# A two-layer hybrid decoder on one core: the low parts of the mixing's weights kept in device memory for the second half of the sequence

## The chip, the core and the metric

The kernel runs on one core of a Trainium2 chip. The metric is device time in microseconds of one execution (lower is better). TensorE is called PE here (PEld is its loading of weights), VectorE is DVE, ScalarE is ACT, GpSimd is POOL and SyncE is SP. SP computes nothing: it issues nearly all DMAs of this kernel, in one queue, in order.

## The reference: what is computed

Two layers over 1024 positions of width 1024, in float32. Cut to what matters:

```python
for l in range(DEPTH):                                   # DEPTH = 2
    shift_m, scale_m, gate_m, shift_f, scale_f, gate_f = split(silu(c) @ ada_w[l] + ada_b[l], 6)
    h = rms_norm(x, g_pre_mix[l]) * (1.0 + scale_m) + shift_m
    q, k, v, u = split(h @ w_in[l] + b_in[l], ...)       # 512, 128, 128 and 512 columns
    attn_out = sliding_window_attention_with_sinks(rotary(q), rotary(k), v, sinks[l])
    pool_out = causal_pool_mixer(u, pool_w[l], pool_scale[l])
    mix = concatenate([attn_out, pool_out], axis=-1) @ w_out[l]
    x = x + gate_m * rms_norm(mix, g_post_mix[l])
    h = rms_norm(x, g_pre_ffn[l]) * (1.0 + scale_f) + shift_f
    f = (silu(h @ w_gate[l]) * (h @ w_up[l])) @ w_down[l]      # inner width 2816
    x = x + gate_f * rms_norm(f, g_post_ffn[l])
```

## The kernel before

**Three products for one.** To keep float32's accuracy with fast matmuls, each operand is split into a high part (ACT rounds it, L220) and a low part (DVE subtracts the high part from the original, L221), and `mm3` (L263, L266, L267) sums high by high, high by low and low by high into one PSUM bank.

**Two halves.** The sequence is worked on in two halves of 512 positions, h = 0 and 1. Each weight tile of the mixing, 128 x 512 floats (256 KB), is therefore used twice in a layer: 8 tiles for the queries (`q_rows`), 4 for keys and values (`kv_rows`), 8 for the pooling's input (`u_rows`) and 16 for the output projection (`wsrc` in `mix_out`), 36 in all. `weight` fetches such a tile: SP loads it into a `raw` tile (L233), and `split` makes `hi` and `lo` of it. It is called anew for each half, so that loading, rounding and subtraction are done 72 times in a layer. `one_ahead` asks for the tile of the next step before the matmuls of this one are written.

**Buffers.** `part` hands out pieces of 512 columns: two `raw` tiles of 2048, three `hi` tiles and three `lo` tiles of 1024 columns. A piece can be written again when all that use its whole tile are done. The pooling mixer's operands and some left operands of the output projection take `lo` pieces too.

**Stages of a layer's mixing**, with the times of layer 0 in the profile:
- first queries, keys and values (q0, kv0; to about 57 us);
- the "dense" stage (to about 158 us): pooling input of half 0 (u0), then queries, keys and values of half 1 (q1, kv1), with the attention of half 0 and its pooling written between them;
- out0 (to about 215 us): output projection of half 0 in two rounds of 8 tiles, beside the first attention blocks of half 1;
- u1 (to about 250 us): pooling input of half 1; the feed-forward's first products follow it, among them out1 (about 305 to 350 us), the output projection of half 1.

**The modulation beside it.** The columns of `ada_w` that this layer still needs are summed on DVE in the dense stage and in out0: `ada_sum` loads tiles `ar` of 256 KB through SP (L306) into two buffers and adds them up (`ada`, L296 and L298). When 8 tiles are summed, the sum is split (`ph<-ada`), and `close` has PE reduce it over the partitions (L412 and L413, or L469 and L470). `after(ins, recent["split"])` keeps each such sum behind the low part that was written last before it.

A scheduler puts the instructions of each engine in order at build time. Each engine then runs its own list strictly in order and waits at semaphores. In the second half, the instruction that needs a free `lo` piece is DVE's subtraction; the SP queue holds loads of `raw`, `ar` and the residual, and stores.

Of the kernel before, what the change touches and what calls it, by code (L numbers as in the profile page):

```python
# [11 lines left out]
F32 = mybir.dt.float32  # L12
# [3 lines left out]
AF = mybir.ActivationFunctionType  # L16
# [4 lines left out]
P = 128  # L21
# [7 lines left out]
ATT = NH * HD  # L29
KVW = NKV * HD  # L30
QK = ATT + KVW
QKV = ATT + 2 * KVW
POOLW = D - ATT
INW = QKV + POOLW
# [32 lines left out]
def hybrid_decoder_kernel(  # L67
# [22 lines left out]
    nc = tc.nc  # L90
# [5 lines left out]
    dr = ctx.enter_context(tc.tile_pool(name="dr", bufs=1, space=DRAM))  # L96
# [19 lines left out]
    def t_(tag, shape, dt=F32):  # L116
        if tag in SMALL:
            return small.tile(shape, dt, tag=tag, name=tag, bufs=SMALL[tag])
        if tag in SHARED:
            return sb.tile(shape, dt, tag=tag, name=tag, bufs=SHARED[tag])  # L120
        return now["pool"].tile(shape, dt, tag=tag, name=tag, bufs=REGIONS[now["name"]][tag])
# [3 lines left out]
    def part(tag, n=512):  # L125

        tile_, used = now.get(tag, (None, WIDE[tag]))
        if used + n > WIDE[tag]:
            tile_, used = t_(tag, [P, WIDE[tag]], F32 if tag == "raw" else F32R), 0
        now[tag] = (tile_, used + n)  # L130
        return tile_[:, used : used + n]
# [84 lines left out]
    recent = {}  # L216

    def split(hi, lo, src):

        a = nc.scalar.activation(hi, src, AF.Copy)  # L220
        v = nc.vector.tensor_sub(lo, src, hi.bitcast(F32))  # L221
        for ins, prev in zip((a, v), recent.get("hold", ())):
            after(ins, prev)
        recent["cast"], recent["split"] = a, v

    def weight(*srcs):

        raw = part("raw")
        for psl, view, src in srcs:
            dst = raw[psl]  # L230
            if view:
                dst = dst.rearrange("p (a b) -> p a b", a=view)
            nc.sync.dma_start(dst, src)  # L233
        hi, lo = part("hi"), part("lo")
        split(hi, lo, raw)
        return hi, lo

    def after(ins, prev):
        tc.add_manual_dep(
            ins.ins, prev.ins.name,  # L240
            mybir.DependencyInfo(mybir.DependencyClass.NoSync, mybir.DependencyReason.DATA),
            reason="order on the same engine",
        )
# [15 lines left out]
    ALLP = slice(0, P)  # L259
# [404 lines left out]
    def natural_proj(fn, left, wsrc, ss, G):  # L664

        K = len(left)  # L670
        lows = {}
        for nh in range(2):
            cs = slice(nh * 512, (nh + 1) * 512)
            banks = [acc_bank() for _ in range(NT)]
            for k in range(K):
                wh, wl = weight(*wsrc(k, nh))
                lh = part("hi")
                if k in lows:
                    ll = lows[k]
                    nc.scalar.activation(lh, left[k], AF.Copy)  # L680
                else:
                    if nh == 0 and k < 6:
                        lows[k] = t_("uT" if k < 4 else "pt", [P, UW], F32R)[:, :T]
                    ll = lows[k] if k in lows else part("lo")
                    split(lh, ll, left[k])
                for t in range(NT):
                    mm3(banks[t], lh[:, tiles[t]], ll[:, tiles[t]], wh, wl, k == 0, k == K - 1)
                yield
            for t in range(NT):
                square_sum(ss, t, nh, banks[t])  # L690
                nc.vector.tensor_mul(fn[t][:, cs], banks[t], G[:, cs])  # L691
# [21 lines left out]

    def kv_rows(l, k):
        return weight(
            (ALLP, 2, w_in[l, k * P : (k + 2) * P, ATT:QKV].rearrange("(a p) n -> p a n", p=P))
        )

    def q_rows(l, k):
        return weight((ALLP, None, w_in[l, k * P : (k + 1) * P, 0:ATT]))  # L720

    def u_rows(l, k):
        return weight((ALLP, None, w_in[l, k * P : (k + 1) * P, QKV:INW]))

    def all_rows(rows, l, step=1):
        return [lambda k=k: rows(l, k) for k in range(0, KD, step)]
# [295 lines left out]
    def mix_out(l, cats, G):  # L1022
        order = [*range(GRP, KD), *range(GRP)]
        left = [cats[k // 4][:, k % 4, :] for k in order]

        def wsrc(i, nh):
            k = order[i]
            cs = slice(nh * 512, (nh + 1) * 512)
            if k < GRP:
                return (  # L1030
                    (slice(0, HD), None, w_out[l, k * HD : (k + 1) * HD, cs]),
                    (slice(HD, P), None, w_out[l, (GRP + k) * HD : (GRP + k + 1) * HD, cs]),
                )
            return ((ALLP, None, w_out[l, k * P : (k + 1) * P, cs]),)

        fn = [t_("fn", [P, D]) for _ in range(NT)]
        ss = t_("ss", [P, 8])
        return fn, ss, natural_proj(fn, left, wsrc, ss, G)
# [346 lines left out]
    scaled = normalise(xs, rstd, cs=FIRST_COLS[0], hold=(recent["row"], recent["hot"]))  # L1385
    recent["hold"] = recent["square"], scaled
    ask_q = one_ahead(all_rows(q_rows, 0))
    recent.pop("hold")

# [20 lines left out]
    queries0 = q_pass(0, hts[0], par, qkvs0, ask_q, second_piece)  # L1410
    normalise(xs, rstd, cs=FIRST_COLS[1], hold=recent["hold"])
    keys0 = kv_pass(0, hts[0], par, qkvs0, one_ahead(all_rows(kv_rows, 0, 2)), (pv, msc_bank()))
    NB0 = len(FIRST_BLOCKS)
    sums = None
# [36 lines left out]
    for l in range(DEPTH):  # L1451
# [14 lines left out]
        def dense0():  # L1466
            yield from q_pass(l, hts[0], par, qkvs[0], ask) if l else queries0
            yield from kv_pass(l, hts[0], par, qkvs[0], ask) if l else keys0

        ask = one_ahead(  # L1470
            (all_rows(q_rows, l) + all_rows(kv_rows, l, 2) if l else [])
            + all_rows(u_rows, l) + all_rows(q_rows, l) + all_rows(kv_rows, l, 2)
        )
        side = ada_jobs(l)
# [43 lines left out]
        ]  # L1518
        pre = first_half()
        ask1 = one_ahead(all_rows(u_rows, l))  # L1520
        run(u_pass(l, 1, pieces, cols, uts[1], lambda k, ins: None, ask1), KD, (att, 10), (pre, NT + 2 + KD))
        pool = pool_mix(l, 1, uts[1], cols, cats[1][1])
# [138 lines left out]
```

## Time and profile before

| | us |
|---|---|
| median of 3 runs | 1906.01 (1905.44 to 1906.4) |
| span of the profiled execution, first to last instruction | 1904.4 |
| PE busy in it | 1864.7 (98%) |
| DVE busy | 1540.4 (81%) |
| ACT busy | 948.4 (50%) |
| POOL busy | 20.0 (1%) |
| moved by DMA | 341.86 MB, 180 GB/s in the mean |

For the profiled execution the page gives the span alone; the median of the timed runs lies 1.6 us above it. PE's matmuls overlap and their ends are modelled, so that 98% is not PE at its best pace: the pace has to be taken from the distance between two matmuls' starts. The shares are means over stages that differ; the mixing's stages are read one by one.

### The profile page before, as it was taken

The page shows a single profiled execution, that of the slowest core. Times are in us where ns is not written, and L with a number is a line of the kernel's source. Part 1 is how long each engine was busy: PE and PEld are TensorE (multiplying, and loading weights), DVE is VectorE, ACT ScalarE, POOL GpSimd, SP SyncE. Part 2 cuts the span into 40 slices and gives each one's busy share as a digit, 9 for nine tenths or more (in the row PEclk, how much of TensorE's full clock was granted, in tenths as well). Part 3 has the DMA queues.
Part 4 walks back from the last instruction along what each step waited for, and adds up shares of the span by engine and source line. Part 5 has one row for each costly group of instructions (what it writes and reads, how often), then busy time and mean ns, then how long its engine had stood idle before and what let it go on. Part 6 is the DMA issues. An engine that isn't in the chain of part 4 may idle for free.

```text
span 1904.4 us, 26019 instructions
## 1 busy us (share of the span) xinstructions
PE 1864.7 (98%) x8954; PEld 1540.3 (81%) x8954; DVE 1540.4 (81%) x2889; ACT 948.4 (50%) x1791; POOL 20.0 (1%) x67
## 2 busy tenths in 40 slices
PE   7999999999999999999999999999999999999998
PEld 5887788888888788888888868888887888888886
DVE  7899886668898888788879988846888888867687
ACT  4875795654222223445558667845622222234452
POOL 0000000000000000000000000000000000000000
PEclk9999999999999999999999989999999999999999
DMA  9345563655555665944554464536654565574343
GB/s 341 112 144 161 161 221 125 191 172 193 194 183 188 205 210 172 320 143 150 172 179 139 126 181 164 178 111 209 214 189 146 198 216 197 199 249 157 117 141 114
DMA packets 229540, 341.86 MB, mean 180 GB/s; under 512 B 17016, under 2 KB 126472, under 8 KB 229408
## 3 DMA queue, kind: packets, MB, share of 16 engines
q1 hardware_dynamic: 228800, 338.10, 53.8%
q10 hardware_dynamic: 576, 2.10, 0.3%
q8 instruction: 70, 1.15, 0.3%
q14 instruction: 62, 0.51, 0.1%
q0 software_dynamic: 32, 0.00, 0.0%
HBM read 267.25 MB, written 72.89 MB: 179 GB/s over the span
## 4 chain that ended last, share of the span: by engine, by line
PE 80%; DVE 10%; DMA 5%; ACT 3%; issue 2%; SPq 0%; DVEq 0%; ACTq 0%; POOL 0%; POOLq 0%
PE acc L263 25%; PE acc L266 24%; PE acc L267 24%; DMA ar<-in_ada_w_dram 2%; DVE lo L221 1%; DVE ada L298 1%; DMA raw<-in_w_up_dram 1%; PE msc L904 1%; PE msc L561 1%; ACT hi L220 1%; PE pv L263 1%; PE pv L266 1%; PE pv L267 1%; ACT raw L554 1%; DVE fn L1162 1%
## 5 line engine op out<-in xcount | busy, mean ns | idle before, releaser
L220 ACT ACTIVATE hi<-raw 128x1024 fp32r<-128x1024 f32 (+1 forms) x388 | 331.8, 868 | 360.1 <-PE acc L266 197.1
L221 DVE TENSOR_TENSOR lo<-raw,hi 128x1024 fp32r<-128x1024 f32 (+1 forms) x388 | 380.2, 987 | 121.3 <-ACT hi L220 116.4
L263 PE MATMUL acc<-t,hi 128*128 128x512 f32 x704 | 274.6, 390 | 2.7 <-ACT hi L220 2.6
L266 PE MATMUL acc<-t,hi 128*128 128x512 f32 x704 | 274.0, 389 | 0.0
L267 PE MATMUL acc<-t,lo 128*128 128x512 f32 x704 | 271.8, 389 | 0.0
L263 PE MATMUL acc<-bh,hi 128*128 128x512 f32 x520 | 202.8, 390 | 0.0
L267 PE MATMUL acc<-bh,lo 128*128 128x512 f32 x520 | 202.4, 389 | 0.0
L263 PE MATMUL acc<-hT,hi 128*128 128x512 f32 x480 | 190.2, 396 | 0.6 <-DVE fn L691 0.6
L266 PE MATMUL acc<-hT,hi 128*128 128x512 f32 x480 | 188.4, 392 | 0.0
L267 PE MATMUL acc<-hT,lo 128*128 128x512 f32 x480 | 187.6, 392 | 0.0
L1162 DVE TENSOR_TENSOR fn<-acc,fn 128x512 f32<-128x512 f32 x220 | 150.3, 685 | 38.2 <-PE acc L267 37.6
L263 PEld LDWEIGHTS acc<-t,hi 128*128 128x128 f32 x704 | 132.2, 188 | 32.1 <-ACT hi L220 5.1
L267 PEld LDWEIGHTS acc<-t,lo 128*128 128x128 f32 x704 | 132.2, 188 | 28.7 <-DVE lo L221 1.2
L266 PEld LDWEIGHTS acc<-t,hi 128*128 128x128 f32 x704 | 132.2, 188 | 27.1
L266 PE MATMUL acc<-ph,hi 128*128 128x512 f32 x320 | 124.7, 390 | 0.0
L1098 ACT ACTIVATE fn<-fn 128x512 f32<-128x512 f32 x44 | 27.9, 633 | 181.7 <-DVE fn L1162 181.7
L263 PEld LDWEIGHTS acc<-bh,hi 128*128 128x128 f32 x520 | 97.6, 188 | 20.2
L267 PEld LDWEIGHTS acc<-bh,lo 128*128 128x128 f32 x520 | 97.6, 188 | 20.2
L298 DVE SCALAR_TENSOR_TENSOR ada<-ar,c_act,ada 128x512 f32<-128x512 f32 x140 | 104.6, 747 | 10.1 <-DMA ar<-in_ada_w_dram 9.7
L263 PE MATMUL acc<-hi 128*128 128x512 f32 x256 | 103.5, 410 | 2.4 <-DVE fn L691 2.0
L263 PEld LDWEIGHTS acc<-hT,hi 128*128 128x128 f32 x480 | 90.2, 188 | 19.2 <-DVE fn L691 1.4
L267 PEld LDWEIGHTS acc<-hT,lo 128*128 128x128 f32 x480 | 90.1, 188 | 18.6 <-issue 0.2
(323 smaller groups left out, 3814.5 us busy)
## 6 DMA issues: line engine op xcount, KB each, us to landing
ar<-in_ada_w_dram SPq DMA_DIRECT2D x160, 256.0 KB
raw<-in_w_gate_dram SPq DMA_DIRECT2D x44, 512.0 KB
raw<-in_w_up_dram SPq DMA_DIRECT2D x44, 512.0 KB
raw<-in_w_in_dram SPq DMA_DIRECT2D x80, 256.0 KB
raw<-keeps SPq DMA_DIRECT2D x40, 512.0 KB
keeps<-fn SPq DMA_DIRECT2D x66, 256.0 KB
two_b<-in_w_down_dram SPq DMA_DIRECT2D x30, 512.0 KB
raw<-keepa SPq DMA_DIRECT2D x25, 512.0 KB
```

Source lines behind the costliest of these rows:

```text
L220: a = nc.scalar.activation(hi, src, AF.Copy)
L221: v = nc.vector.tensor_sub(lo, src, hi.bitcast(F32))
L263: ins = nc.tensor.matmul(dst, lh, rh, start=first, stop=False)
L266: nc.tensor.matmul(dst, lh, rl, start=False, stop=False)
L267: return nc.tensor.matmul(dst, ll, rh, start=False, stop=last)
L298: ins = nc.vector.scalar_tensor_tensor(acc, w, c_act[:, i : i + 1], acc, op0=ALU.mult, op1=ALU.add)
L554: nc.scalar.activation(hf, bank, AF.Identity, bias=shift, scale=scale)
L561: ins = nc.tensor.transpose(bank[:, t * P : (t + 1) * P], src[t], ident)
L904: nc.tensor.transpose(bank[:, i * P : (i + 1) * P], s[:, ii, ck * P : (ck + 1) * P], ident)
L1098: nc.scalar.activation(g, g, AF.Silu)
L1162: nc.vector.tensor_add(halves_of(dst)[m], bank, halves_of(src)[m])
```

## The change

The first call of `weight` for a tile now also stores the low part to a buffer in device memory, by a DMA in POOL's queue. The second call, for half 1, loads the low part from there by SP, into its `lo` piece, and only ACT's rounding is left to compute. Tiles are told apart by a key; both layers use the same 36 buffers. The tile of the weight itself is loaded in both halves, as before. In all 72 stores and 72 loads of 256 KB come in, and 72 subtractions of 128 x 512 on DVE go (20 of them lie in q1, kv1 and u1 of each layer, 16 in out1).

```diff
+    low_parts = {}
+
-    def weight(*srcs):
+    def weight(key, *srcs):
...
             nc.sync.dma_start(dst, src)
         hi, lo = part("hi"), part("lo")
+        if key in low_parts:
+            nc.sync.dma_start(lo.bitcast(F32), low_parts.pop(key))
+            recent["cast"] = nc.scalar.activation(hi, raw, AF.Copy)
+            return hi, lo
         split(hi, lo, raw)
+        low_parts[key] = kept_low = dr.tile([P, 512], F32, tag=f"low{key[1:]}", name="low", bufs=1)
+        nc.gpsimd.dma_start(kept_low, lo.bitcast(F32))
         return hi, lo
...
-        return weight((ALLP, None, w_in[l, k * P : (k + 1) * P, 0:ATT]))
+        return weight((l, "q", k), (ALLP, None, w_in[l, k * P : (k + 1) * P, 0:ATT]))
```

`kv_rows`, `u_rows` and `wsrc` get keys in the same way. Since the second half no longer calls `split`, `recent["split"]` stays at an older instruction there, and the scheduler also reorders the work around it. (Lines of the changed kernel are numbered 2 higher in `weight` and about 8 higher behind it.)

In DVE's list of layer 0, at the end of kv1 (`qkv<-acc` is the eviction of the keys and values, `rt` the rotary's products), before:

```order
L298 SCALAR_TENSOR_TENSOR ada<-ar,c_act,ada 128x512 x2
L749 TENSOR_TENSOR qkv<-acc,bqkv 128x256 x4
L795 TENSOR_TENSOR rt<-qkv,cos_t 128x80
L796 TENSOR_TENSOR rt<-qkv,sin_t 128x80
L298 SCALAR_TENSOR_TENSOR ada<-ar,c_act,ada 128x512
L797 TENSOR_TENSOR rt<-qkv,cos_t 128x80
L298 SCALAR_TENSOR_TENSOR ada<-ar,c_act,ada 128x512
L798 TENSOR_TENSOR rt<-qkv,sin_t 128x80
```

and now:

```order
L306 SCALAR_TENSOR_TENSOR ada<-ar,c_act,ada 128x512
L757 TENSOR_TENSOR qkv<-acc,bqkv 128x256 x2
L306 SCALAR_TENSOR_TENSOR ada<-ar,c_act,ada 128x512
L757 TENSOR_TENSOR qkv<-acc,bqkv 128x256 x2
L221 TENSOR_TENSOR ph<-ada,ph 128x512
L803 TENSOR_TENSOR rt<-qkv,cos_t 128x80
L304 TENSOR_SCALAR ada<-ar,c_act 128x512
```

The modulation's sums stand two tiles further ahead of the eviction: the split `ph<-ada` that closes a sum comes right behind the eviction, where before two more tiles had to be added first. Between this eviction and the end of out0, 26 tiles were left to add in layer 0 and 24 are now; in layer 1 it was 22 and is 20.

In SP's queue at the end of the dense stage of layer 0 (`gate` is the finished modulation row, `lo<-low` the new load), before:

```order
L473 DMA gate<-ar 1x512
L306 DMA ar<-in_ada_w_dram 128x512 x2
L482 DMA G<-gate 128x1024
L306 DMA ar<-in_ada_w_dram 128x512 x4
L233 DMA raw<-in_w_out_dram 128x512
L233 DMA raw<-in_w_out_dram 64x512 x6
L306 DMA ar<-in_ada_w_dram 128x512 x7
```

and now:

```order
L481 DMA gate<-ar 1x512
L314 DMA ar<-in_ada_w_dram 128x512
L238 DMA lo<-low 128x512
L314 DMA ar<-in_ada_w_dram 128x512
L238 DMA lo<-low 128x512
L490 DMA G<-gate 128x1024
L314 DMA ar<-in_ada_w_dram 128x512 x2
L238 DMA lo<-low 128x512
L314 DMA ar<-in_ada_w_dram 128x512
L238 DMA lo<-low 128x512
L314 DMA ar<-in_ada_w_dram 128x512
L235 DMA raw<-in_w_out_dram 128x512
```

The four low parts of kv1 stand between the loads of `ar` and ahead of the output projection's weights. A load of a low part waits in this queue until PE has read what its `lo` tile held before, and what stands behind it waits with it.

In POOL's list of layer 0, from the copies of the halo of half 0 to that of half 1 (`vz` are zeros for the attention's values, `uT<-halo` the pooling's margin), before:

```order
L781 COPY halo<-uT 128x16 x2
L808 CAST vz<-vz_zero 128x64 x6
L784 COPY uT<-halo 128x16
L808 CAST vz<-vz_zero 128x64 x4
L784 COPY uT<-halo 128x16 x3
```

and now:

```order
L789 COPY halo<-uT 128x16 x2
L816 CAST vz<-vz_zero 128x64 x4
L243 DMA low<-lo 128x512
L816 CAST vz<-vz_zero 128x64 x2
L243 DMA low<-lo 128x512 x8
L792 COPY uT<-halo 128x16
L243 DMA low<-lo 128x512 x6
L816 CAST vz<-vz_zero 128x64 x2
L243 DMA low<-lo 128x512
L816 CAST vz<-vz_zero 128x64 x2
L792 COPY uT<-halo 128x16 x3
```

The 16 stores of out0 stand among copies that wait for PE, and those copies stand behind stores.

More of the change, by code (lines that the diff above doesn't have):

```diff
@@ L715, in kv_rows @@
         return weight(
-            (ALLP, 2, w_in[l, k * P : (k + 2) * P, ATT:QKV].rearrange("(a p) n -> p a n", p=P))
+            (l, "kv", k), (ALLP, 2, w_in[l, k * P : (k + 2) * P, ATT:QKV].rearrange("(a p) n -> p a n", p=P))
         )
     def q_rows(l, k):
-        return weight((ALLP, None, w_in[l, k * P : (k + 1) * P, 0:ATT]))
+        return weight((l, "q", k), (ALLP, None, w_in[l, k * P : (k + 1) * P, 0:ATT]))
     def u_rows(l, k):
-        return weight((ALLP, None, w_in[l, k * P : (k + 1) * P, QKV:INW]))
+        return weight((l, "u", k), (ALLP, None, w_in[l, k * P : (k + 1) * P, QKV:INW]))
     def all_rows(rows, l, step=1):
@@ L1030, in wsrc @@
                 return (
+                    (l, "o", i, nh),
                     (slice(0, HD), None, w_out[l, k * HD : (k + 1) * HD, cs]),
@@ L1033, in wsrc @@
                 )
-            return ((ALLP, None, w_out[l, k * P : (k + 1) * P, cs]),)
+            return (l, "o", i, nh), (ALLP, None, w_out[l, k * P : (k + 1) * P, cs])
         fn = [t_("fn", [P, D]) for _ in range(NT)]
```

## The prediction

> **What bounds the kernel now.** I read the page's shares first, then busy time by stretch, then what the matmuls of a stretch need at PE's own pace, and last the chain of waits in the stretches that the change touches.
>
> ```profile
> PE 1864.7 (98%) x8954; PEld 1540.3 (81%) x8954; DVE 1540.4 (81%) x2889; ACT 948.4 (50%) x1791; POOL 20.0 (1%) x67
> 93.00:158.00 65.00, 64.67 (x417) 56.30 (x417) 61.80 (x172) 48.00 (x123) 3.33 (x11) 1.00 0.43 131
> 158.00:215.00 57.00, 52.38 (x247) 40.47 (x245) 50.88 (x138) 36.80 (x92) 0.28 (x1) 0.94 0.65 194
> 215.00:245.00 30.00, 29.63 (x168) 24.66 (x168) 27.07 (x79) 24.70 (x66) 0.45 (x2) 1.00 0.46 158
> 305.00:350.00 45.00, 45.00 (x199) 36.73 (x198) 21.48 (x33) 22.77 (x44) 0.00 (x0) 1.00 0.34 107
> 1020.00:1095.00 75.00, 74.40 (x479) 64.62 (x478) 71.09 (x203) 57.22 (x148) 3.59 (x11) 1.00 0.47 140
> 1095.00:1150.00 55.00, 50.85 (x238) 38.88 (x236) 47.12 (x130) 33.36 (x82) 0.70 (x1) 0.91 0.60 179
> ```
>
> The columns of a stretch are its length, then busy time of PE, PEld, DVE, ACT and POOL, the granted clock, the share of the DMA engines and GB/s. In layer 0 they are q1 with kv1, out0, u1 and out1; the last two are q1 with kv1 and out0 of layer 1. DVE is busy 95% of the dense stretches (61.80 of 65, 71.09 of 75) and only 48% of out1. PE looks full nearly everywhere, so I take its need from the pace at which matmuls follow one another without a wait, 0.23 us for 512 columns and 0.12 us for 256:
>
> ```profile
> 202.54 0.23 PE acc L266
> 203.78 0.12 PE pv L267
> ```
>
> Matmuls of 512 columns, in the stretch 93 to 158 (three groups) and in out0 (five groups):
>
> ```profile
> L263 PE MATMUL acc<-hi,hT 128*128 128x512 f32 x32 | 12.8, 400 | 0.0
> L266 PE MATMUL acc<-lo,hT 128*128 128x512 f32 x32 | 12.8, 399 | 0.0
> L267 PE MATMUL acc<-hi,hT 128*128 128x512 f32 x32 | 12.5, 391 | 0.0
> ...
> L266 PE MATMUL acc<-lo,hi 128*128 128x512 f32 x52 | 21.2, 415 | 0.0
> L263 PE MATMUL acc<-hi 128*128 128x512 f32 x51 | 21.1, 426 | 0.8 <-DVE fn L691 0.8
> L267 PE MATMUL acc<-hi,uT 128*128 128x512 f32 x32 | 12.0, 400 | 0.0
> L267 PE MATMUL acc<-hi,pt 128*128 128x512 f32 x12 | 4.6, 400 | 0.0
> L267 PE MATMUL acc<-hi,lo 128*128 128x512 f32 x8 | 3.1, 391 | 0.0
> ```
>
> Dense: 96 x 0.23 + (417 - 96) x 0.12 = 60.6 of 65 us, so PE leaves 4.4 us of room there although DVE is full. Out0: 155 x 0.23 + (247 - 155) x 0.12 = 46.7 of 57, room 10.3. In u1 and out1 PEld is busy 82% of the stretch (24.66 of 30, 36.73 of 45), and PE 99% and 100%: I read no room. So out0 is where time lies about, and the chain through it says why. These are the loads of `ar` on the chain, three in the dense stage and five in out0, start and length:
>
> ```profile
> 101.30 3.96 DMA ar<-in_ada_w_dram
> 106.76 3.50 DMA ar<-in_ada_w_dram
> 131.12 3.74 DMA ar<-in_ada_w_dram
> 158.53 2.97 DMA ar<-in_ada_w_dram
> 174.50 3.79 DMA ar<-in_ada_w_dram
> 182.92 4.11 DMA ar<-in_ada_w_dram
> 187.91 3.45 DMA ar<-in_ada_w_dram
> 210.16 3.39 DMA ar<-in_ada_w_dram
> ```
>
> The five take 17.7 of out0's 57 us. The loop is: DVE adds a tile, which frees one of two `ar` buffers, SP loads the next, DVE waits or works on, and PE's evictions and closing matmuls stand behind the sums. Out0 goes at the pace of the modulation, not at that of its own matmuls.
>
> **The change part by part.** What DVE does in these stretches (the first two rows are from 93 to 158, then out0, then u1):
>
> ```profile
> L221 DVE TENSOR_TENSOR lo<-raw,hi 128x512 fp32r<-128x512 f32 x12 | 8.1, 683 | 0.0
> L894 DVE TENSOR_SCALAR sb<-sb,st 128x256 f32<-128x256 f32 x18 | 5.2, 341 | 0.0
> ...
> L298 DVE SCALAR_TENSOR_TENSOR ada<-ar,c_act,ada 128x512 f32<-128x512 f32 x24 | 18.0, 750 | 4.1 <-DMA ar<-in_ada_w_dram 4.0
> ...
> L221 DVE TENSOR_TENSOR lo<-raw,hi 128x512 fp32r<-128x512 f32 x10 | 6.8, 685 | 1.2 <-ACT hi L220 1.2
> ```
>
> *Dense, per layer.* Twelve subtractions of 0.683 us go: 8.2 us of a full DVE. PE has 4.4 us of room, and two more tiles of modulation now stand in this stage (1.5 us of DVE). Ends 0 and -4.4; I take -1.5, nearer to none, since PE's 60.6 us leave out the 512-column matmuls of smaller groups.
>
> *Out0, per layer.* Nothing is removed here, but two tiles fewer are left to add (26 to 24, 22 to 20 by the order). At 57 us for some 27 tiles (24 rows of L298 and a first one for each sum) a tile is worth 2.1 us, and in layer 1, with 23 tiles in 55 us, 2.4: two are 4.2 to 4.8. Ends 0 (the tiles are ahead in the list and not in time) and -10.3 (all of PE's room); I take -4.5. Late next would be PE itself.
>
> *u1 and out1, per layer.* Eight subtractions of 0.685 us in u1, 5.5 us, beside a PE without room: ends 0 and -5.5, I take -0.5. Sixteen in out1 with DVE busy 21.48 of 45: covered by PE's stream, 0. Should that cover go, DVE has the other half of the stretch.
>
> *The traffic, per layer.* 36 stores and 36 loads of 256 KB. They run beside the `ar` loads, which took 2.97 us when little else was under way and up to 4.11. Ends: 0, and all eight chain loads 1.14 us longer, +9.1. Half the out0 stores will fall between `ar` loads, so I take 0.25 us on each of the eight, +2. The Trainium skill, page "DMA: Bandwidth & Descriptors", section "Issuing engines are not separate DMA queues", speaks against the change here: DMAs started by POOL run on the same 16 engines as SP's and interleave with them, so the other queue takes them out of nobody's way. By that rule the end of 0 is not to be had; no row shows it, for POOL's queue moves 4 KB in this trace.
>
> *SP's queue.* What waits where now:
>
> ```profile
> SPq L306 <- DVE ada L298: 93.8, 79, 9.8
> SPq L233 <- DVE lo L221: 83.9, 25, 11.8
> DVE ada L298 <- DMA ar<-in_ada_w_dram: 9.7, 22, 1.1
> ```
>
> (total us, times, longest.) A load of a low part waits until PE has read its tile, and the `ar` loads queue behind it; DVE's sums wait for those, and the attention behind the sums. Today's waits of mixing loads are 3.4 us each (83.9 / 25), SP stands still in them and DVE feels 9.7 us of all that. Twelve dense loads share six tiles: ends 0 and 6 x 3.4 = 20 us of SP, of which a third on DVE, +7. The three `lo` tiles let a load go some four weights ahead of its matmuls, so I take +0.5. The issues themselves are covered by SP's idle time.
>
> *POOL's queue.* The rows for what stands there:
>
> ```profile
> 1.27 1.01 POOL L146 DMA_DIRECT2D pos_i<-in_positions_dram  x1 [0.33 <-issue]
> 118.90 0.51 POOL L808 CAST vz<-vz_zero 128x64 fp32r<-128x64 f32 x2 [15.45 <-PE pv L266]
> 200.99 0.28 POOL L784 COPY uT<-halo 128x16 f32<-128x16 f32 x1 [43.04 <-PE acc L267]
> ```
>
> A store costs POOL about 1.01 us, 72 us in all, beside 1884 us of idling. The copies wait long for PE, so six stores of out0 stand behind the halo copy of 200.99 and hold their `lo` tiles until then; a tile comes up again three tiles later, which is two weights before the end of out0. A copy held up by stores is one to three us late, and zeros are wanted one attention block, some 20 us, later. I take 0. Without that cover the split of a late output weight would wait.
>
> *The start, once.* Twelve stores fall into the first 57 us, where the DMA engines are full:
>
> ```profile
> 20.00:30.00 10.00, 9.65 (x48) 6.71 (x46) 9.09 (x19) 6.42 (x12) 0.00 (x0) 1.00 1.08 387
> ACT hi L220 <- DMA raw<-in_w_in_dram: 1.4, 1, 1.4
> ```
>
> At 387 GB/s a store takes 0.68 us of all engines, twelve 8.1: ends 0 and +8.1. In the first 60 us one wait of 1.4 us is for a weight (second row), so I take +1.
>
> *Sum.* Per layer -1.5 - 4.5 - 0.5 + 2 + 0.5 = -4.0; two layers -8, the start +1: -7. The profiled execution has 1904.4 us of span and would have 1897.4; the median of the runs lies 1.6 above that span: **1899 us**.
>
> **The rivals.**
>
> *Freed DVE time is lost (25%).* Against a gain speaks that PE needs 60.6 of the dense 65 us, and that the order of a list makes nothing earlier if the `ar` loads still take 3.5 us in turn. Then out0 keeps its 57 us: dense -1.5, traffic +2, SP +0.5 a layer, start +1: 1906.0 + 3 = 1909, or 1904.5 if half of out0's term comes after all; I put it at 1907, between them.
>
> *The stores stretch the `ar` loop of out0: slower (13%).* One mechanism: 16 stores of 4.2 MB run within 57 us on engines that are already 65% busy, each round of two tiles lengthens, and PE waits for the closing matmuls. Without the traffic a layer gains 6.0; with 12 rounds in out0 it decides when a round is 0.5 us longer. At 1.14 us (2.97 to 4.11) on 9 of 12 rounds a layer loses 10.3 - 6.0 = 4.3: 1906.0 + 8.6 + 1 = 1915.6. For it speaks the chain; against it, that DVE waited for `ar` just 4.0 us in all of out0.
>
> *SP stands before the low parts: slower (10%).* If +7 is reached in place of +0.5, a layer gives 7 - 4.5 = +2.5: 1906.0 + 5 + 1 = 1912. From 4 us per layer on, 0.7 on each of six waits, nothing is gained.
>
> *POOL and DVE hold one another up (2%).* If a DVE instruction of the L894 kind (5.2 of 65 us) could not run while POOL prepares a store, 36 stores x 1.01 x 8% cost a layer at most 3 us: 1905. The Trainium skill, page "SBUF — State Buffer", section "SBUF: two separate sides", tells of such a lock between DVE's two-port forms and descriptors written by POOL; no row here shows it, as POOL idles beside DVE.
>
> That the subtractions do not go can be left out: the list of DVE holds 95 of them at 128x512 with the change, 167 without.
>
> **How the numbers follow.** My forecast's case (1890 to 1903) gets 50%. About 0.2%, 3.8 us, is what a measurement of this kernel can tell from no change: 1902.2 to 1909.8 is "same". The forecast gives faster almost whole, the first and last rivals are mostly same, the two others slower; a few per cent of the first rival fall to either side: faster 0.52, same 0.25, slower 0.23. The range of 1890 to 1914 reaches from all of out0's two tiles and half of dense's room to the SP rival; beyond it lie a tenth on either side, the stretched loop above.
>
> **What would show it.** Right: out0 (from the first output weights to the second round's evictions) 3 to 5 us shorter in each layer, the `ar` loads there below 4 us, DVE below 90% in the dense stretches, out1 unchanged. Wrong: `ar` loads of 4 us and more on the chain, SP's waits for PE at the new loads with DVE waiting behind, or a later end of kv1. The forecast fails first if DVE's freed time does not bring the modulation forward.

## The result and the profile after

The changed kernel takes 1919.74 us (median of 4 runs, 1916.27 to 1920.8), the kernel before in the same sitting 1906.2: a ratio of 1.0063, 95% interval 1.005 to 1.0075. By that ratio it is about 12 us slower; the two medians lie 13.5 us apart. (Below, a loss in us is the ratio's share of the median before.) The forecast was 1899, 7 us faster, with 1914 as its upper end.

The page of the profile after, the lines that answer to those of before: busy times, the two DMA queues, the shares of the chain, the sums of the modulation.

```profile
PE 1866.3 (97%) x8954; PEld 1541.9 (80%) x8954; DVE 1499.9 (78%) x2817; ACT 946.2 (49%) x1791; POOL 53.7 (3%) x139
...
q1 hardware_dynamic: 239168, 356.98, 56.4%
q0 software_dynamic: 5792, 18.88, 2.6%
...
PE 78%; DVE 9%; DMA 7%; ACT 4%; issue 2%; SPq 0%; DVEq 0%; ACTq 0%
...
L306 DVE SCALAR_TENSOR_TENSOR ada<-ar,c_act,ada 128x512 f32<-128x512 f32 x140 | 104.8, 748 | 23.4 <-DMA ar<-in_ada_w_dram 22.6
```

DVE is busy 40.5 us less (1540.4 to 1499.9), as planned, and PE's work is the same, but the span is 13.3 us longer (1917.7 against 1904.4). POOL's queue moves 18.88 MB where it moved 4 KB. In the chain DMA has 7%, before 5%. DVE's wait ahead of the sums of `ada` is 23.4 us; before it was 10.1:

```profile
L298 DVE SCALAR_TENSOR_TENSOR ada<-ar,c_act,ada 128x512 f32<-128x512 f32 x140 | 104.6, 747 | 10.1 <-DMA ar<-in_ada_w_dram 9.7
```

Neither of the two is a price by itself. Of the versions below, run 2 has DMA at 7% of its chain and run 3 waits 16.3 us at these sums, and neither is slower than before; run 8 has 4% and 16.6 us and is slower by 7.4 us.

Busy time by stretch, after: the dense stage (its end is about 1 us later than before), out0 with the start of u1, out1, and out0 of layer 1, in the columns of the prediction.

```profile
95.00:160.00 65.00, 64.30 (x420) 56.19 (x419) 56.11 (x161) 48.40 (x125) 2.68 (x12) 1.00 0.57 178
162.00:235.00 73.00, 66.14 (x330) 52.22 (x329) 58.20 (x160) 46.70 (x119) 8.74 (x18) 0.95 0.74 241
315.00:360.00 45.00, 45.00 (x200) 36.85 (x199) 12.01 (x17) 22.09 (x42) 0.00 (x0) 1.00 0.64 198
1105.00:1180.00 75.00, 67.06 (x337) 53.98 (x336) 57.98 (x160) 47.35 (x121) 9.77 (x18) 0.95 0.69 224
```

The same two stretches of out0, before:

```profile
162.00:235.00 73.00, 68.69 (x342) 54.08 (x343) 64.58 (x184) 50.97 (x126) 0.73 (x3) 0.95 0.56 170
1105.00:1180.00 75.00, 72.45 (x367) 57.83 (x366) 63.19 (x175) 51.81 (x133) 1.18 (x3) 0.95 0.53 165
```

DVE's load fell in all of them (56.11 of 65 us in the dense stage, 12.01 of 45 in out1), and PE did less in the same time: 66.14 us against 68.69, and 67.06 against 72.45. The rate of the DMAs in out0 rose from 170 to 241 GB/s.

Where the time went is read from the evictions. For a source line: count, shortest, median and longest in ns, first and last start in us. DVE's eviction of the output projection, before (second round of out0, second round of out1, second round of out0 in layer 1):

```profile
L691 DVE TENSOR_TENSOR fn<-acc,G x4: 691/692/692, 226.7 to 228.9; 128x512 f32<-128x512 f32 x4
...
L691 DVE TENSOR_TENSOR fn<-acc,G x4: 681/682/683, 354.5 to 357.4; 128x512 f32<-128x512 f32 x4
...
L691 DVE TENSOR_TENSOR fn<-acc,G x4: 691/692/692, 1163.3 to 1165.5; 128x512 f32<-128x512 f32 x4
```

and after:

```profile
L699 DVE TENSOR_TENSOR fn<-acc,G x4: 680/692/692, 230.5 to 234.7; 128x512 f32<-128x512 f32 x4
...
L699 DVE TENSOR_TENSOR fn<-acc,G x4: 682/682/684, 360.4 to 363.3; 128x512 f32<-128x512 f32 x4
...
L699 DVE TENSOR_TENSOR fn<-acc,G x4: 680/692/692, 1176.0 to 1180.3; 128x512 f32<-128x512 f32 x4
```

ACT's eviction of u0 in layer 1, before and then after:

```profile
L777 ACT ACTIVATE uT<-acc,cols x4: 669/686/706, 1033.5 to 1037.9; 128x512 f32<-128x512 f32 x4
```

```profile
L785 ACT ACTIVATE uT<-acc,cols x4: 672/686/702, 1044.4 to 1048.8; 128x512 f32<-128x512 f32 x4
```

DVE's eviction of the keys and values of half 1 in both layers, before and then after:

```profile
L749 DVE TENSOR_TENSOR qkv<-acc,bqkv x4: 406/406/409, 158.4 to 159.4; 128x256 f32<-128x256 f32 x4
...
L749 DVE TENSOR_TENSOR qkv<-acc,bqkv x4: 415/416/420, 1093.0 to 1095.3; 128x256 f32<-128x256 f32 x4
```

```profile
L757 DVE TENSOR_TENSOR qkv<-acc,bqkv x4: 413/416/417, 159.4 to 161.0; 128x256 f32<-128x256 f32 x4
...
L757 DVE TENSOR_TENSOR qkv<-acc,bqkv x4: 416/416/418, 1105.2 to 1107.2; 128x256 f32<-128x256 f32 x4
```

| first eviction of | before | after | later by |
|---|---|---|---|
| kv1, layer 0 | 158.4 | 159.4 | 1.0 |
| out0, second round | 226.7 | 230.5 | 3.8 |
| out1, second round | 354.5 | 360.4 | 5.9 |
| u0, layer 1 | 1033.5 | 1044.4 | 10.9 |
| kv1, layer 1 | 1093.0 | 1105.2 | 12.2 |
| out0, layer 1, second round | 1163.3 | 1176.0 | 12.7 |

The losses lie in out0 of layer 0 (2.8 us), behind it up to out1 (2.1), from there to u0 of layer 1 (5.0) and from u0 to kv1 there (1.3); out0 of layer 1 is only 0.5 us longer. Stores run in most of these stretches, but none between out0 and out1, and the length of a stretch also differs by 1 to 2.5 us between executions that take the same time in all (behind run 16). The dense stage of layer 0, which lost twelve subtractions of 0.683 us, gains nothing. The loads of `ar` on the chain in out0, start and length:

```profile
155.47 3.12 DMA ar<-in_ada_w_dram
...
160.80 2.77 DMA ar<-in_ada_w_dram
...
173.01 4.50 DMA ar<-in_ada_w_dram
...
182.26 3.74 DMA ar<-in_ada_w_dram
...
207.14 5.84 DMA ar<-in_ada_w_dram
...
213.86 3.63 DMA ar<-in_ada_w_dram
```

Before, the five in out0 took 2.97 to 4.11 us; now there is one of 4.50 and one of 5.84. The next question was which of the change's parts costs this: bytes, queues, order, or lost cover.

### The profile page after: what moved, and what is told of

It reads as the page before. It is cut to its first block, busy times and chain, and to the rows that moved or that the text cites. A ratio compares the mean times of both kernels' runs of the same rounds, so it can differ in the third digit from the quotient of the medians.

```text
span 1917.7 us, 26230 instructions
## 1 busy us (share of the span) xinstructions
PE 1866.3 (97%) x8954; PEld 1541.9 (80%) x8954; DVE 1499.9 (78%) x2817; ACT 946.2 (49%) x1791; POOL 53.7 (3%) x139
## 3 DMA queue, kind: packets, MB, share of 16 engines
q0 software_dynamic: 5792, 18.88, 2.6%
## 4 chain that ended last, share of the span: by engine, by line
PE 78%; DVE 9%; DMA 7%; ACT 4%; issue 2%; SPq 0%; DVEq 0%; ACTq 0%
PE acc L271 24%; PE acc L274 24%; PE acc L275 24%; DMA ar<-in_ada_w_dram 3%; DVE ada L306 1%; DMA raw<-in_w_up_dram 1%; DVE lo L221 1%; PE msc L912 1%; DMA raw<-in_w_in_dram 1%; PE msc L569 1%; ACT hi L220 1%; ACT sb L896 1%; PE pv L271 1%; PE pv L274 1%; PE pv L275 1%
## 5 line engine op out<-in xcount | busy, mean ns | idle before, releaser
L220 ACT ACTIVATE hi<-raw 128x1024 fp32r<-128x1024 f32 (+2 forms) x316 | 287.4, 922 | 314.2 <-PE acc L274 183.5
L221 DVE TENSOR_TENSOR lo<-raw,hi 128x1024 fp32r<-128x1024 f32 (+2 forms) x316 | 331.2, 1056 | 76.4 <-ACT hi L220 74.4
L306 DVE SCALAR_TENSOR_TENSOR ada<-ar,c_act,ada 128x512 f32<-128x512 f32 x140 | 104.8, 748 | 23.4 <-DMA ar<-in_ada_w_dram 22.6
L271 PEld LDWEIGHTS acc<-hT,hi 128*128 128x128 f32 x480 | 90.6, 189 | 19.5 <-DVE fn L699 1.4
L274 PEld LDWEIGHTS acc<-hT,hi 128*128 128x128 f32 x480 | 90.6, 189 | 16.9
```

The costliest lines, as they stand in the source:

```text
L271: ins = nc.tensor.matmul(dst, lh, rh, start=first, stop=False)
L274: nc.tensor.matmul(dst, lh, rl, start=False, stop=False)
L306: ins = nc.vector.scalar_tensor_tensor(acc, w, c_act[:, i : i + 1], acc, op0=ALU.mult, op1=ALU.add)
```

## The experiments

Sixteen kernels ran, each beside the kernel before. Its median was 1906.5 to 1907.6 us there, so that 0.1% is 1.9 us. Theories at the start: **traffic** (stores and loads lengthen the loads that the loop of `ar` waits for), **SP's queue** (SP stands at loads of low parts while `ar` and `raw` queue up behind it) and **order** (the scheduler's other order of DVE and ACT costs the time).

**1. The stores alone.**

```diff
         if key in low_parts:
-            nc.sync.dma_start(lo.bitcast(F32), low_parts.pop(key))
-            recent["cast"] = nc.scalar.activation(hi, raw, AF.Copy)
+            low_parts.pop(key)
+            split(hi, lo, raw)
             return hi, lo
```

> The 72 stores alone: the second half subtracts as before, nothing is loaded, so 18.9 MB of stores more (36 stores of 256 KB a layer) and no DVE time freed. Traffic theory (stores and loads stretch the ar loads, which are longer in the dense stage, and freed DVE time is worth little): about half the loss is the stores', +5 to +9 us on before, 1911 to 1915. SP-queue theory (the loss comes from SP standing at loads of low parts): stores do nothing, 1905 to 1908. Order theory (the loss comes from the changed order of DVE's and ACT's lists in the second half): nothing either, 1905 to 1908.

Measured 1915.16 us, ratio 1.0038 (1.0025 to 1.0051): 7.2 us of loss (7.7 between the medians) without any load. ACT's list is that of before, and 2867 of DVE's 2889 instructions stand in its order. Neither of the other theories has this.

**2. The loads alone.**

```diff
-            nc.sync.dma_start(lo.bitcast(F32), low_parts.pop(key))
+            nc.sync.dma_start(lo.bitcast(F32), low_parts.pop(key) and one_low[0])
...
-        nc.gpsimd.dma_start(kept_low, lo.bitcast(F32))
+        if not one_low:
+            one_low.append(dr.tile([P, 512], F32, tag="low", name="low", bufs=1))
+            nc.gpsimd.dma_start(one_low[0], lo.bitcast(F32))
```

> The 72 loads and the freed subtractions without the stores (36 loads a layer, all from one buffer that is stored once; the values of the low parts are left out). Traffic theory: half the traffic's loss stays, 1909 to 1914. SP-queue theory: the whole loss stays, 1917 to 1921, since SP stands at the same loads. Order theory: 1917 to 1921 as well.

Measured 1906.79 us, ratio 0.9995 (0.9983 to 1.0007). The loads through SP, with the subtractions gone and the lists reordered, cost nothing in the whole. It is less than the traffic theory expected as well. In the trace this nothing is a sum of gains and a loss. The evictions of kv1 and of out0's second round, layer 0 and then layer 1:

```profile
L759 DVE TENSOR_TENSOR qkv<-acc,bqkv x4: 412/414/425, 158.3 to 160.0; 128x256 f32<-128x256 f32 x4
...
L701 DVE TENSOR_TENSOR fn<-acc,G x4: 680/690/690, 223.2 to 227.5; 128x512 f32<-128x512 f32 x4
...
L759 DVE TENSOR_TENSOR qkv<-acc,bqkv x4: 414/416/418, 1096.1 to 1097.8; 128x256 f32<-128x256 f32 x4
...
L701 DVE TENSOR_TENSOR fn<-acc,G x4: 678/690/691, 1163.9 to 1168.2; 128x512 f32<-128x512 f32 x4
```

From the one to the other out0 takes 64.9 and 67.8 us, before 68.3 and 70.3. The dense stage of layer 1 is 3.6 us longer than before (table behind run 16), and there SP's stand at a low part is on the chain, with a late tile of `w_in` behind it:

```profile
1025.46 0.34 SPq L238
1025.89 0.37 SPq L316
1026.36 4.73 DMA raw<-in_w_in_dram
```

The changed kernel has the same at 1034 us, with a load of 5.65 us.

**3. Freed DVE time and nothing else.**

```diff
         if key in low_parts:
-            nc.sync.dma_start(lo.bitcast(F32), low_parts.pop(key))
+            low_parts.pop(key)
             recent["cast"] = nc.scalar.activation(hi, raw, AF.Copy)
-            return hi, lo
+            return hi, hi
```

> The second half neither subtracts, loads nor stores a low part; its matmuls take the high part twice (the low parts' values are left out). This is the freed DVE time by itself, with the reordered lists. Traffic and SP-queue theories: everything the change frees and nothing that it adds, 1895 to 1904. Order theory: 1912 or more, since the reordered lists are what costs. If freed DVE time is worth nothing: 1905 to 1907.

Measured 1906.07 us, ratio 0.999 (0.9978 to 1.0001). This is the ceiling of the whole idea: 72 subtractions and their waits are worth 2 us (by the interval, between 4 and nothing), within what a measurement can tell from no change. In the trace something does come: the evictions of the second round of out0 and of out1 in layer 0,

```profile
L700 DVE TENSOR_TENSOR fn<-acc,G x4: 678/691/692, 223.9 to 228.1; 128x512 f32<-128x512 f32 x4
...
L700 DVE TENSOR_TENSOR fn<-acc,G x4: 678/682/683, 354.1 to 357.1; 128x512 f32<-128x512 f32 x4
```

are 2.8 us and 0.4 us earlier than before (226.7 and 354.5). Out0 did get shorter, and the feed-forward behind it took most of that back. One part of it is the granted clock. The same 10 us in this kernel, and then in the kernel before, with two stretches beside it:

```profile
265.00:275.00 10.00, 9.71 (x45) 8.20 (x46) 7.41 (x19) 8.53 (x21) 0.27 (x1) 0.83 0.61 181
```

```profile
190.00:200.00 10.00, 7.85 (x32) 5.59 (x31) 9.32 (x22) 6.66 (x16) 0.00 (x0) 0.83 0.50 145
265.00:275.00 10.00, 8.79 (x50) 7.26 (x49) 8.34 (x19) 10.00 (x24) 0.15 (x1) 1.00 0.59 183
1130.00:1140.00 10.00, 8.72 (x23) 6.06 (x23) 9.76 (x24) 5.12 (x15) 0.70 (x1) 0.66 0.62 175
```

At a clock of 0.83, 10 us lack 1.7 us. Before, a dip stands in out0 (190 to 200) and none at 265; here one stands at 265, where PE is busy 9.71 of 10 us, and out0 has none. So a part of out0's 2.8 us may be a dip that now falls elsewhere; one trace of each does not show more.

**4. The loads in POOL's queue.**

```diff
-            nc.sync.dma_start(lo.bitcast(F32), low_parts.pop(key))
+            nc.gpsimd.dma_start(lo.bitcast(F32), low_parts.pop(key))
```

> The whole change, with the loads of low parts in POOL's queue in place of SP's, so that ar and raw loads no longer stand behind them. SP-queue theory: most of the loss goes, 1900 to 1909. Traffic theory: the loss stays, 1915 to 1922, since the same bytes move at nearly the same time. Order theory: 1917 to 1922.

Measured 1921.66 us, ratio 1.0066 (1.0043 to 1.009). The whole loss stays although `ar` and `raw` stand behind no load of a low part. In the changed kernel SP did wait at them (total us, times, longest):

```profile
SPq L238 <- PE acc L275: 50.8, 27, 4.2
...
SPq L238 <- PE msc L275: 14.7, 2, 8.1
```

65.5 us in all. The loads alone wait as long and are not slower in the whole, and in POOL's queue the loss stays, so SP's queue does not make the loss. Nor is the dense stage of layer 1 shorter here, where that wait stood on the chain (run 2): 101.3 us from kv0 to kv1, 98.8 in the changed kernel.

**5. Stores of 1/64 of the bytes.** As run 1, with 8 columns of 512.

```diff
-        nc.gpsimd.dma_start(kept_low, lo.bitcast(F32))
+        nc.gpsimd.dma_start(kept_low[:, :8], lo.bitcast(F32)[:, :8])
```

> As the stores alone (72 stores from POOL, the second half subtracts, nothing is loaded), but each store takes 8 columns of 512: 128 pieces of 32 bytes in place of 128 of 2 KB, so POOL does the same work and waits at the same places while the bytes are 1/64. Byte theory (the 7.7 us of the stores alone are bytes and the longer loads beside them): 1904 to 1909. Queue theory (POOL's work on the stores, its waits, and the lo pieces held until POOL comes round): 1911 to 1917.

Measured 1907.58 us, ratio 0.9996 (0.9985 to 1.0007). POOL does the same work at the same places, and the loss is gone. Out0 here:

```profile
162.00:235.00 73.00, 67.68 (x345) 53.11 (x346) 65.30 (x184) 51.34 (x128) 9.25 (x18) 0.98 0.56 173
```

POOL is as busy as with whole stores, and DVE and the DMA rate are as before.

**6. The stores in ACT's queue.** As run 1, with `nc.scalar` in place of `nc.gpsimd`.

> As the stores alone, but issued in ACT's queue in place of POOL's. Byte theory: 1911 to 1917, as from POOL, plus what ACT loses where it waits for DVE's subtraction ahead of a store. Queue theory: the loss that is POOL's goes, 1904 to 1909, unless ACT's waits take its place.

Measured 1916.35 us, ratio 1.0043 (1.0029 to 1.0057). Another queue, the same loss. This is what the Trainium skill, page "DMA: Bandwidth & Descriptors", section "Issuing engines are not separate DMA queues", says: the queue that starts a DMA only saves the issuing engine's time, and the DMAs run on the same 16 engines. The two runs agree with it (0.38% and 0.43%).

**7. All stores, a second half that neither subtracts nor loads.** As run 3, with the stores of the change.

> All 72 stores, and a second half that neither subtracts nor loads a low part (its matmuls take the high part twice; the low parts' values are left out). The stores alone cost 0.38%, the loads alone nothing, both together 0.63 to 0.66%: what is the rest? If loads and stores cost more together than apart, this is without it: 1910 to 1915. If the stores cost more once DVE's list is reordered and shorter, the loss of the whole change is here too: 1917 to 1922.

Measured 1915.77 us, ratio 1.0042 (1.0027 to 1.0057). The reordered and shorter list neither adds to the stores' loss nor takes anything from it.

**8. The stores of out0 alone** (16 of 36 a layer).

```diff
-        nc.gpsimd.dma_start(kept_low, lo.bitcast(F32))
+        if key[1] == "o":
+            nc.gpsimd.dma_start(kept_low, lo.bitcast(F32))
```

> Of the stores alone just the 16 a layer of the output projection's weights (32 in all, 8.4 MB of 18.9), which fall into out0. Stretched-loop theory (the stores cost where ar loads and stores meet in out0): most of the 7.7 us, 1910 to 1914. If they cost in proportion to their bytes: 3.4 us, 1909 to 1911. If the 12 stores at the start of a layer and the 8 of u0 carry the loss: 1905 to 1908.

Measured 1914.32 us, ratio 1.0039 (1.0027 to 1.0052): as much as all stores. 8.4 MB in two stages of some 57 us cost 7.4 us, and the other 10.5 MB little (1.9 us, run 13). Out0, and three of the six loads of `ar` on its chain:

```profile
162.00:235.00 73.00, 65.76 (x316) 51.47 (x317) 60.01 (x162) 45.90 (x111) 8.95 (x18) 0.93 0.70 224
```

```profile
176.45 4.74 DMA ar<-in_ada_w_dram
...
185.82 5.29 DMA ar<-in_ada_w_dram
...
208.82 5.08 DMA ar<-in_ada_w_dram
```

The rate is 224 GB/s against 170. These three loads take 4.7 to 5.3 us and the other three 3.0 to 4.0, where before the five took 2.97 to 4.11.

**9 and 10. A third `ar` buffer**, in the kernel before and in the changed one.

```diff
-    SMALL = dict(junk=1, st=12, rs=8, ss=4, halo=8, rows=1, cols=2, colp=4, sk=2)
-    SHARED = dict(hT=8, fn=4, raw=2, hi=3, lo=3, sa=2, sb=2, ar=2, ada=1, ph=3, G=1)
+    SMALL = dict(junk=1, st=12, rs=8, ss=4, halo=4, rows=1, cols=1, colp=4, sk=2)
+    SHARED = dict(hT=8, fn=4, raw=2, hi=3, lo=3, sa=2, sb=2, ar=3, ada=1, ph=3, G=1)
```

> The kernel before with three ar buffers in place of two (the room comes from halo, 8 to 4, and cols, 2 to 1). If out0 goes at the pace of the loop of ar loads, as the prediction has it: 1898 to 1903. If PE's own work and its evictions set the pace of out0, so that freed DVE time and earlier modulation are worth nothing: 1905 to 1909.

> The whole change with three ar buffers, made as in the kernel before it. If the stores cost by stretching the ar loads of out0, one more buffer hides most of that: 1906 to 1913. If they cost in another way (the weights' own loads, or accesses to memory beside them): 1916 to 1921.

Measured: before with three 1905.15 us, ratio 0.9998 (0.9985 to 1.001); after with three 1910.74 us, ratio 1.0029 (1.0015 to 1.0042). Chain shares by line between 158 and 230 us, the kernel before and then with three buffers:

```profile
by line: DMA ar<-in_ada_w_dram 24.6%; DVE ada L298 10.9%; PE acc L266 8.9%; PE acc L267 8.1%; PE acc L263 7.9%; ACT junk L501 3.9%; DVE fn L691 3.6%; issue 3.5%; DVE lo L221 3.4%; DVE ph L221 2.7%; PE msc L866 2.2%; PE msc L904 1.9%; PE msc
```

```profile
by line: PE acc L263 18.7%; PE acc L266 18.3%; PE acc L267 17.8%; ACT junk L501 6.2%; PE msc L904 3.7%; DVE ada L298 2.8%; issue 2.7%; PE msc L866 2.7%; PE msc L867 2.3%; PE pv L267 2.2%; PE pv L263 2.1%; PE pv L266 2.0%; PE msc L846 1.7%; 
```

The loads of `ar`, 24.6% of this stretch of the chain, are no longer among its costliest lines. Out0 does get shorter by it, as the evictions of kv1 and of out0's second round show, layer 0 and then layer 1, in the kernel before with three buffers:

```profile
L749 DVE TENSOR_TENSOR qkv<-acc,bqkv x4: 413/416/424, 160.1 to 161.8; 128x256 f32<-128x256 f32 x4
...
L691 DVE TENSOR_TENSOR fn<-acc,G x4: 690/691/692, 225.6 to 227.8; 128x512 f32<-128x512 f32 x4
...
L749 DVE TENSOR_TENSOR qkv<-acc,bqkv x4: 412/416/418, 1098.5 to 1100.4; 128x256 f32<-128x256 f32 x4
...
L691 DVE TENSOR_TENSOR fn<-acc,G x4: 690/691/692, 1164.4 to 1166.6; 128x512 f32<-128x512 f32 x4
```

Out0 takes 65.5 and 65.9 us, with two buffers 68.3 and 70.3. But the time of the whole is the same, since other stretches are longer. The kernel differs by more than the buffer (`halo` and `cols` shrink, and the scheduler orders DVE's list anew), so that what makes them longer is not shown; what is shown is that a gain in this stage need not reach the end. DVE's wait ahead of the sums, with three buffers before and after:

```profile
L298 DVE SCALAR_TENSOR_TENSOR ada<-ar,c_act,ada 128x512 f32<-128x512 f32 x140 | 104.3, 745 | 2.6 <-DMA ar<-in_ada_w_dram 2.1
```

```profile
L306 DVE SCALAR_TENSOR_TENSOR ada<-ar,c_act,ada 128x512 f32<-128x512 f32 x140 | 104.3, 745 | 7.5 <-DMA ar<-in_ada_w_dram 7.0
```

In the changed kernel the third buffer takes the wait from 23.4 to 7.5 us and more than half of the loss with it (0.63% to 0.29%). So this loop carries a good part of the stores' cost, though a quicker loop gave the kernel before nothing. Out0 then takes 66.1 and 64.6 us, as in the kernel before with three buffers; the loss that is left lies outside out0, and no run shows by which way it comes.

**11 and 12. The change for one weight matrix alone.** `w_out` alone (below), and `w_in` alone with the condition reversed; the other is split twice.

```diff
         split(hi, lo, raw)
+        if not (key[1] == "o"):
+            return hi, lo
         low_parts[key] = kept_low = ...
```

> The change for the 16 tiles of w_out alone (16 stores in out0, 16 loads in out1, a layer); the others are split twice as before. The stores of out0 cost 0.39% alone, and out1 has PE busy throughout: 1912 to 1916 if the loads of out1 are free. If the rest of the whole change's loss comes from them: 1917 to 1921.

> The change for the 20 tiles of w_in alone (stores at the start and in u0, loads in q1, kv1 and u1, a layer); w_out's are split twice as before. By the stores alone and the loads alone, both near nothing there: 1904 to 1909. If stores and loads meet to cost more than each apart, in u0 and the dense stage: 1909 to 1913. The prediction's gains, were they real without out0's stores: 1895 to 1902.

Measured: `w_out` 1911.02 us, 1.0034 (1.002 to 1.0049); `w_in` 1911.01 us, 1.0023 (1.0012 to 1.0035). The two parts add up to 0.57%, near the whole. For `w_out` the stores explain it all (run 8: 0.39%). The part for `w_in`, which holds all the gains that were forecast outside out1, is a loss by itself, which neither its stores (run 1 less run 8) nor the loads (run 2) led one to expect.

**13 to 15. What of `w_in`'s loss is what.** The stores of `w_in` alone (run 8 with `!=`); its stores and a second half that neither subtracts nor loads its low parts (run 7 with `if key[1] == "o": return hi, lo` ahead of the store); run 12 with three `ar` buffers.

> The stores of w_in's low parts alone (20 a layer, at the start and in u0); the second half subtracts and loads nothing. If the loss of the w_in part (1911.0, +0.23%) is the stores': 1909 to 1912. If it takes the loads as well: 1905 to 1908.

> The stores of w_in's low parts, and a second half that neither subtracts nor loads these 20 low parts (its matmuls take the high part twice; the low parts' values are left out); w_out is split twice as before. If the loss needs the loads: 1903 to 1907. If it is the stores': 1907 to 1912.

> The change for w_in alone with three ar buffers. If its loss goes through the ar loop, as half of the whole change's does: 1902 to 1907, at best faster than before, since DVE's freed time is then all that is left. If it goes through the weights' own loads in the first and the u0 stage: 1908 to 1912.

Measured: 1909.31 us, 1.001 (0.9999 to 1.002); 1907.47 us, 1.0 (0.999 to 1.001); 1910.29 us, 1.0016 (1.0007 to 1.0024). The stores alone cost 0.1%, which the interval does not tell from nothing; with the freed time added nothing is left of it; with the loads as well it is 0.23% (run 12). So this part's loss needs the loads, which without stores cost nothing in the whole (run 2). The dense stage of layer 1, from kv0 to kv1, takes 100.9 us in run 12 and 96.8 in run 14, which loads nothing. The third buffer leaves it open: 0.16% is inside the interval of run 12.

**16. Stores as in the change, but all loads from one buffer.**

```diff
-            nc.sync.dma_start(lo.bitcast(F32), low_parts.pop(key))
+            nc.sync.dma_start(lo.bitcast(F32), low_parts.pop(key) is not None and one_low[0])
...
         nc.gpsimd.dma_start(kept_low, lo.bitcast(F32))
+        if not one_low:
+            one_low.append(dr.tile([P, 512], F32, tag="one", name="low", bufs=1))
+            nc.gpsimd.dma_start(one_low[0], lo.bitcast(F32))
```

> The whole change, all stores as it has them, but all loads read one buffer that is stored once (the values of the low parts are left out). If loads and stores together cost more than apart because both are under way: the whole loss, 1917 to 1921. If reading back many buffers is what the loads alone lacked: as the stores without loads, 1912 to 1916.

Measured 1918.39 us, ratio 1.0062 (1.0044 to 1.0079), the whole loss. Reading back many buffers is not the cause. Loads and stores together cost about 0.2% more than the stores without loads, in two pairs (1.0063 against 1.0042, 1.0023 against 1.0). Each difference is hardly larger than its uncertainty, but the traces say where it may come from.

**Where the time of each part lies.** The same evictions cut each profiled execution into stretches (us; one execution of each kernel, each row up to the first eviction named):

| stretch | before | freed time alone (3) | loads alone (2) | stores alone (1) | whole change | before, three buffers (9) |
|---|---|---|---|---|---|---|
| start to kv1, layer 0 | 158.4 | 158.3 | 158.3 | 160.1 | 159.4 | 160.1 |
| to out0, second round | 68.3 | 65.6 | 64.9 | 72.3 | 71.1 | 65.5 |
| to out1, second round | 127.8 | 130.2 | 129.5 | 127.7 | 129.9 | 129.0 |
| to kv0, layer 1 | 644.1 | 645.9 | 645.4 | 644.6 | 646.0 | 647.2 |
| to kv1, layer 1 (dense) | 94.4 | 95.5 | 98.0 | 96.3 | 98.8 | 96.7 |
| to out0, second round | 70.3 | 69.7 | 67.8 | 70.6 | 70.8 | 65.9 |
| to the end | 741.1 | 740.7 | 741.0 | 741.8 | 741.7 | 740.2 |

Small differences are scatter: runs 5 and 13, whose whole time is that of before within their intervals, have 67.7 and 66.9 us in out0 of layer 0 and 646.6 and 646.2 on the way to kv0 of layer 1. Two things are larger than that. The dense stage of layer 1 takes 98.0 to 101.3 us in all five kernels with two `ar` buffers that load the low parts of `w_in` (runs 2, 4, 12 and 16 and the whole change), and 93.8 to 96.8 in all ten that do not. And the whole change is 12.8 us longer than the loads alone, of which the two out0 have 9.2. So the loads cost some 3 us in layer 1, which run 2's shorter out0 hides; the stores take that gain of out0 away, and then it shows. By these traces that is most of what stores and loads cost together and neither alone; no run tests it by itself.

No version that ran is faster than the kernel before beyond its measurement, and by run 3 there are about 2 us to be had.

## Why the prediction was wrong

- **Out0, -4.5 a layer: the step that failed.** The sum takes what out0 gains for what the kernel gains, and lets out0 keep its gain beside the stores. Neither holds. "Out0 goes at the pace of the modulation" is borne out as far as single traces go: without stores out0 is shorter with freed DVE time (2.7 and 0.6 us in run 3, 3.4 and 2.5 in run 2) and with a quicker loop (2.8 and 4.4 in run 9). But run 3 gains 2 us in the whole, where the terms of out0, dense and u1 made 13 in two layers, and runs 2 and 9 gain nothing: the other stretches are longer by about as much. Why they are is open, but for the granted clock, which explains at most a part. In the changed kernel out0 is not shorter at all but 2.8 and 0.5 us longer, where 3 to 5 us shorter was to show the forecast right, since the stores lengthen it (see the traffic below).
- **Dense, -1.5, and u1, -0.5: too large in sum.** DVE at 95% with PE 4.4 us short of full was not a bound: kv1 comes 1.0 us later in layer 0, and even with the freed time alone it comes at 158.3 us, before 158.4.
- **The traffic, +2 a layer: mis-sized.** The stores alone cost 3.6 us a layer (run 1), nearly all by those of out0 (run 8), and the lengthening is 1 us and more on some loads where 0.25 on each was taken. Set against the loads alone, the whole change's out0 is 6.2 and 3.0 us longer. The mechanism, longer `ar` loads in out0, is the rival "the stores stretch the loop", given 13%. Its 1915.6 came from 10.3 us of cost and 6.0 of gain a layer; measured are about 3.7 and 1. That rival was nearer by the mechanism than by its sum.
- **SP's queue, +0.5: right that it is small.** In the whole SP's 65.5 us of waits at the new loads cost nothing (run 2), and the loss stays without them (run 4), so the rival built on them is refuted as the cause. The term is right by a sum that it did not foresee: the loads do lengthen the dense stage of layer 1 by some 3 us, and out0 gains as much. A wait of SP stands on the chain there, but with the loads in POOL's queue the stage is no shorter, so that the mechanism is open.
- **POOL, 0: right.** A store takes POOL 541 ns, not the 1.01 us assumed:

```profile
L243 POOL DMA_DIRECT2D low<-lo x72 | 39.0, 541 | 941.3 <-DVE lo L221 923.1 <-DVE sb L902 7.7 <-DVE rs L517 4.8
```

Its work, its place in the list and any lock with DVE together cost nothing (run 5).
- **The start, +1: right within what can be told** (run 13, 0.1% for the stores of the start and of u0 together).
- **The rival "freed DVE time is lost" was right on its half**: the freed time is worth 2 us (run 3). Its sum of +3 us had the traffic at +2 a layer, as the forecast did, and so fell short of 12.
- **Not in the prediction:** 4 us that stores and loads cost together and neither alone (table behind run 16).
- **Signs of being wrong** that the prediction named and that came: `ar` loads of 4.50 and 5.84 us on the chain, and a later end of kv1.
- **The range** ended at 1914 because the cases of cost were each set against gains of 6 us a layer that were not there.

## What to carry to other kernels

A chain of waits names what came last, not what the time would be without it: before counting on a stage's pace, take the suspect away in the kernel as it is (here one more buffer: out0 2.8 and 4.4 us shorter, the kernel no faster) and read the ceiling from a version that leaves out the work. A stage that ends earlier is no gain until the end of the kernel shows it, and a part that costs nothing in the whole may hide a loss behind a gain: compare the stages too. Extra bytes were not free on DMA engines that are 56% busy when a loop with two buffers waits for each load: price them by the loads they lengthen, in the stage where they fall, and give the loop another buffer first. Moving such DMAs to another engine's queue changed nothing here (runs 4 and 6).

## What the runs showed of the hardware

- **Stores hurt where they meet loads that are waited for.** 32 stores of 256 KB in out0 cost 7.4 us; 40 others 1.9 us (interval from 0 to 3.8). 72 loads of the same size, most of them in other stages, cost nothing in the whole without stores. Whether as many loads in out0 would cost what the stores do there was not run.
- **The granted clock dips in steps of about 1.7 us.** In stretches of 10 us it is mostly 1.00, at some places 0.83 or 0.66 (rows under run 3): the clock lacks 1.7 or 3.4 us. Read so, without the start and the last 10 us, the dips of a profiled execution sum to between 3.4 us (runs 2, 5, 10 and 15) and 10.4 us (run 8), and they lie in other places from version to version. The Trainium skill, page "TensorE: Matmul & The Clock Gate", section "What's actually happening", has windows of 3.4 us at half rate; an estimate from that page is 1.7 us lacking for one window, and the rows agree. A whole run of one kernel varies by some 10 us (1902.7 to 1912.2 over 25 runs of the kernel before), and the time goes with the clock: over the 112 runs of the kernel before that stood beside the experiments, the mean is 1909.7 us in the 12 with a granted clock of 0.994, 1907.0 in the 39 with 0.996 and 1904.8 in the 15 with 0.998. That dips make the difference is likely by this, but no run sets them.
